# Moving the first two PSUM copies of each down-projection ahead of the silus, and the rotary tables to a later place in the code

## The chip, the cores and the metric

The kernel runs on one core of a Trainium2 chip. The metric is device time in microseconds (us). The time before is a median of 2068.57 us over three runs (2067.76 to 2076.04). A profiled execution of the same program took 2069.25 us; the profile's span, from the first instruction to the last, is 2067.5 us of it.

The core's engines work side by side, each through a list of its own in order: PE multiplies matrices into PSUM, ACT (ScalarE) and DVE (VectorE) work element by element, SP issues the loads. An engine waits for another one by a semaphore, and whatever stands behind the waiting instruction on that engine waits with it.

## The reference

One encoder layer over 256 positions of width 2048, in float32: a half-step SwiGLU feed-forward, a mixer (Fourier branch and grouped attention with a rotation of q and k), and a second half-step feed-forward.

```python
def _swiglu(x, w_gate, w_up, w_down):
    return (jax.nn.silu(x @ w_gate) * (x @ w_up)) @ w_down

h = x + 0.5 * rms_norm(swiglu(rms_norm(x, pre_g), w_gate, w_up, w_down), post_g)   # D_FF = 5632
h = h + rms_norm(merge(gates, attention(u), fourier(u)) @ w_out, post_g)           # u = rms_norm(h); u @ w_in
y = h + 0.5 * rms_norm(swiglu(rms_norm(h, pre_g2), ...), post_g2)
```

## The kernel before

**Precision and weights.** Each float32 matrix is split in two parts, hi and lo, and a product takes three matmuls (L108 to L110: hi·hi, lo·hi, hi·lo). A *piece* of weights is 128x1024: SP loads it into `raw`, ACT copies it to `whi` (L102), DVE subtracts to get `wlo` (L103).

**A round of the feed-forward.** The 5632 inner columns are cut in 11 blocks of 512. The first two are done plainly. The other nine, in each of the two feed-forwards, are rounds: 18 rounds in all. A round has two parts.

- `swiglu` multiplies the 256 tokens (two halves t = 0 and 1) with the gate and up columns of the block. Five of the eight pairs of row blocks use seven products instead of eight, with sums on DVE (`seven`, L557); three are plain. Nine partial results lie in PSUM: `p1, p5, p7` in one pool and `u0, g0, p6, g1, u1` in the pool `pmm`, which has five banks. At the end DVE adds them up (L562): first `x2 <- p6, x1`, then three sums with p7 and p5, then `x1 <- g0`, `x3 <- g1`, and at last the two of `u0, u1`. ACT does the silu of x1 and x3 (L570), DVE the product (L574).
- `Rows.feed` multiplies the block before (transposed, `hT`) with its rows of the down weights and adds that to `y`, in four column blocks `cb` of eight matmul triples. The sum is kept in SBUF: `seed` copies y of a column block into two PSUM banks (ACT, L640, one copy for each half t), PE adds onto them (tile `pr`), `out` copies the banks back to y (ACT, L657).

**What sets the order.** In the rounds DVE, ACT and PE keep the order of the program text. It is made by `Line`: a queue of six pieces. Each `feed` first takes the oldest piece, emits its matmuls (`use`) and the list of work that hangs on it (`then`), and then prepares the new piece (load, `whi`, `wlo`). So a piece is made ready six pieces before it is used, and the work in a `then` list stands between two of these preparations on ACT and DVE. The lists at the end of `swiglu` are `sums` (hung on the last two pieces of pair 6), `gates` (on the gate piece of pair 7) and `ups` (on its up piece). The next piece's matmuls are those of the down-projection's first column block, which need the first two copies; the call of `seed` for these stands at the end of `gates`, behind the two silus.

**Between the first feed-forward and the mixer.** `last_rows` ends the feed-forward: the norm, the residual and the first projection of the mixer, whose weights' pieces are prepared in between. After it SP loads q's and k's gains (`gq, gk`) and the cosine and sine tables (`rc, rsn`), and DVE multiplies them to the four tables `gcq, gsq, gck, gsk` (twelve small instructions, L784 and L787), which `norm_rope` reads later. Here a scheduler decides where DVE's instructions outside the hand-ordered part stand.

Of the kernel before, what the change touches and what calls it, by code (L numbers as in the profile page):

```python
# [10 lines left out]
F32 = mybir.dt.float32  # L11
# [3 lines left out]
AF = mybir.ActivationFunctionType  # L15
ALU = mybir.AluOpType
AX = mybir.AxisListType

P = 128
# [37 lines left out]
def encoder_layer(  # L57
# [48 lines left out]
    def mm3(ps, lh, ll, rh, rl, first, last, onto=False):  # L106

        T.matmul(ps, lh, rh, start=first, stop=False, skip_group_check=onto)  # L108
        T.matmul(ps, lh, rl, start=False, stop=False, skip_group_check=onto)  # L109
        return T.matmul(ps, ll, rh, start=False, stop=last, skip_group_check=onto)  # L110
# [245 lines left out]
    def cbs(a, cb):  # L356
        return a[:, cb * NB:(cb + 1) * NB]
# [175 lines left out]
    def swiglu(line, forms, w, hs, seed):  # L533


        ps, begun, x = {}, set(), {}

        def mul(n, a, b, last=False):
            if n not in ps:
                ps[n] = ptr.tile([P, NB], F32, tag="tr", name="pc") if n in ("p5", "p7", "p1") else                     pmm.tile([P, NB], F32, tag="mm", name="pc")  # L540
            mm3(ps[n][:], *a, *b, n not in begun, last)
            begun.add(n)

        def raw(pair, i):
            return raw_piece(w[pair // 2], pair % 2 * 2 + i)

        def plain(pair, i, *then):
            def use(b):
                for t in range(NT):
                    for j in range(2):  # L550
                        k = 2 * pair + j
                        mul("gu"[i] + str(t), forms.plain[k][t], b[j], k == KD - 1)

            line.feed(lambda: ring(raw(pair, i)[:]), use, *then)

        def minus(out, a, b):
            V.tensor_tensor(out=out, in0=a, in1=b, op=ALU.subtract)  # L557

        def add(out, a, b):
            if out not in x:  # L560
                x[out] = work(out)
            V.tensor_tensor(out=x[out][:], in0=ps[a][:], in1=x[b][:], op=ALU.add)  # L562

        def copy():
            x["x1"] = work("x1")
            A.activation(x["x1"][:], ps["p1"][:], AF.Copy)

        def silu(t):
            g = x["x" + "13"[t]]
            A.activation(g[:], g[:], AF.Silu)  # L570

        def times(t):
            g, up = x["x" + "13"[t]], x["x" + "25"[t]]
            V.tensor_tensor(out=up[:], in0=up[:], in1=g[:], op=ALU.mult)  # L574
            hs.append(up)

        def seven(pair, between=None, *then):
            a11, a12, na22, s1, s2, s3, s4 = forms.seven[pair]
            end = pair == BY_SEVEN[-1]
            h = {}  # L580

            def first():
                ra, rb = raw(pair, 0), raw(pair, 1)
                t = chunk.tile([P, WP, NB], F32, tag=("ch_hi", "ch_lo")[BY_SEVEN.index(pair) % 2], name="t13")
                h.update(ra=ra, rb=rb, t=t)
                minus(t[:, 0, :], ra[:, 1, :], ra[:, 0, :])
                minus(t[:, 1, :], rb[:, 0, :], ra[:, 1, :])
                b = ring(rb[:])
                minus(ra[:, 1, :], rb[:, 0, :], t[:, 0, :])
                return b  # L590

            def second():
                b = ring(h["t"][:])
                minus(h["t"][:, 0, :], h["ra"][:, 1, :], h["rb"][:, 1, :])
                return b

            def two(n, a, m, b, last):
                def use(ws):
                    mul(n, a, ws[0], last)
                    mul(m, b, ws[1], last)  # L600
                return use

            line.feed(first, two("u0", s4, "g0", a12, False))
            line.feed(second, two("p5", s1, "p7", s3, end))
            if between:
                between()
            line.feed(lambda: ring(h["ra"][:]), two("p1", a11, "p6", s2, end), *then[0:2])
            line.feed(lambda: ring(h["t"][:, 0:1, :]), lambda ws: mul("g1", na22, ws[0]), *then[2:])

        sums = [copy, lambda: add("x2", "p6", "x1"), lambda: add("x3", "p7", "x2"), lambda: add("x2", "p5", "x2"),  # L610
                lambda: add("x5", "p5", "x3")]
        gates = [lambda: add("x1", "g0", "x1"), lambda: add("x3", "g1", "x3"), lambda: silu(0), lambda: silu(1),
                 seed]
        ups = [lambda: add("x2", "u0", "x2"), lambda: times(0), lambda: add("x5", "u1", "x5"), lambda: times(1)]
        for kg in range(KD // CK):
            a, b = 2 * kg, 2 * kg + 1
            if kg == KD // CK - 1:
                seven(a, None, *sums)
                plain(b, 0, *gates)
                plain(b, 1, *ups)  # L620
            elif b in BY_SEVEN:
                seven(a)
                seven(b)
            else:
                seven(a, lambda: plain(b, 0))
                plain(b, 1)

    class Rows:
# [2 lines left out]
        def __init__(self, w, rb, y, first):  # L631
            self.w, self.rb, self.y, self.first, self.ps = w, rb, y, first, {}

        def seed(self, cb):
            if cb == D // NB:
                return
            self.ps[cb] = [pmm.tile([P, NB], F32, tag="mm", name="pr") for _ in range(NT)]
            if not self.first:
                for t in range(NT):
                    A.activation(self.ps[cb][t][:], cbs(self.y[t], cb), AF.Copy)  # L640

        def feed(self, line, ch, ahead):

            def use(b, cb, i):
                if i == 0:
                    if cb in ahead:
                        ahead[cb]()
                    self.seed(cb + 1)
                for t in range(NT):
                    for j in range(WP):  # L650
                        k = i * WP + j
                        mm3(self.ps[cb][t][:], ch[0][:, k, t * P:(t + 1) * P], ch[1][:, k, t * P:(t + 1) * P], *b[j],
                            self.first and k == 0, k == CK - 1, not self.first)

            def out(cb):
                for t in range(NT):
                    A.activation(cbs(self.y[t], cb), self.ps[cb][t][:], AF.Copy)  # L657

            for cb in range(D // NB):
                for i in range(CK // WP):  # L660
                    line.feed(lambda i=i, cb=cb: ring(raw_piece(self.w[self.rb, cb], i)[:]),
                              lambda b, i=i, cb=cb: use(b, cb, i), *([lambda cb=cb: out(cb)] if i == CK // WP - 1 else []))

    def ffn(u, rs, wg, wu, wgu, wd, yname, tail, gate0, w_next=None, early=()):
# [30 lines left out]
        with tc.manual_schedule(engines={mybir.EngineType.DVE, mybir.EngineType.Activation, mybir.EngineType.PE}):  # L695
            for f in range(PLAIN, nblk + 1):
                if f == 4:
                    norm, nxt = tail(y)

                def ahead(hs=hs, f=f):  # L700
                    chs.append(new_chunk("hT")) if f > PLAIN else None
                    turn_h(chs[-1], hs)

                before = {D // NB - 1: ahead}
                if f == PLAIN:
                    before[0] = lambda: forms.chunk(KD // CK - 1)
                if f == PLAIN:
                    rows = Rows(wd, 0, y, True)
                    rows.seed(0)
                rows.feed(line, chs[-1] if f > PLAIN else chs[0], before)  # L710
                if f < nblk:
                    hs = []
                    rows = Rows(wd, f - 1, y, False)
                    swiglu(line, forms, wgu[f - PLAIN], hs, lambda rows=rows: rows.seed(0))
            line.end()
        return last_rows(chs[-1], wd, nblk - 1, y, norm, nxt, w_next), nxt

# [59 lines left out]
    load(rc[:], rope_cos)  # L777
    load(rsn[:], rope_sin)
    tabs = {}
    for nm, g in (("q", gq), ("k", gk)):  # L780
        gc = const.tile([P, NT, HD], F32, name="gc" + nm)
        gs = const.tile([P, NT, HD], F32, name="gs" + nm)
        for t in range(NT):
            V.tensor_tensor(out=gc[:, t, :], in0=rc[:, t, :], in1=g[:], op=ALU.mult)  # L784
            v = lambda a: a.rearrange("p (a h c) -> p a h c", a=2, h=2)
            for half in range(2):
                V.tensor_tensor(out=v(gs[:, t, :])[:, :, half, :], in0=v(rsn[:, t, :])[:, :, half, :],  # L787
                                in1=v(g[:])[:, :, 1 - half, :], op=ALU.mult)
        tabs[nm] = (gc, gs)

    def norm_rope(ps, nm, t):

# [305 lines left out]
            V.tensor_tensor(out=cbs(mB[t], cb), in0=w[:], in1=cbs(mB[t], cb), op=ALU.mult)  # L1098


    pv = col_block(u, w_in, 5, between=[nxt.finish, None, lambda: fold_tokens(0)])
    for t in range(NT):
        vt = work("vt")
        A.activation(vt[:], pv[t][:], AF.Copy, scale=rs[t][:, 0:1])
# [225 lines left out]
```

## Time and profile before

| | before |
|---|---|
| median of three runs | 2068.57 us |
| profiled execution | 2069.25 us |
| its span | 2067.5 us |
| PE busy | 2007.7 us (97%) |
| DVE busy | 1711.6 us (83%) |
| ACT busy | 1329.6 us (64%) |
| waiting of PE for the copies of L640 | 40.8 us in 18 pieces |

How to read the profile. The page gives the busy time of each engine over the span. A group of instructions is one line: engine, operation, what it writes and reads, how often, busy time, the mean of one in ns, and the idle time of the engine just before them with what ended it. The view of waits sums these idle times by who waited for whom (total us, times, longest). The timeline lists instructions in order of time; a bracket at a row's end is the idle time before it and what ended that. The view by windows gives, for each stretch of time, its length, the busy time of each engine (with the number of instructions), the granted clock of PE and the load of the DMA engines. The end of a matmul is modelled: back to back, matmuls of one size start every 0.23 us and are shown 0.39 us long, so lengths of stalls are best taken from start to start.

### The profile page before, as it was taken

The page shows a single profiled execution, that of the slowest core. Times are in us where ns is not written, and L with a number is a line of the kernel's source. Part 1 is how long each engine was busy: PE and PEld are TensorE (multiplying, and loading weights), DVE is VectorE, ACT ScalarE, POOL GpSimd, SP SyncE. Part 2 cuts the span into 40 slices and gives each one's busy share as a digit, 9 for nine tenths or more (in the row PEclk, how much of TensorE's full clock was granted, in tenths as well). Part 3 has the DMA queues.
Part 4 walks back from the last instruction along what each step waited for, and adds up shares of the span by engine and source line. Part 5 has one row for each costly group of instructions (what it writes and reads, how often), then busy time and mean ns, then how long its engine had stood idle before and what let it go on. Part 6 is the DMA issues. An engine that isn't in the chain of part 4 may idle for free.

```text
span 2067.5 us, 26007 instructions
## 1 busy us (share of the span) xinstructions
PE 2007.7 (97%) x9200; PEld 1659.1 (80%) x9200; DVE 1711.6 (83%) x2298; ACT 1329.6 (64%) x1898; POOL 28.6 (1%) x30
## 2 busy tenths in 40 slices
PE   9999999999999999999999999999999999999998
PEld 7887777877778778888888888888778777877776
DVE  6898888888888788887877895877888889888885
ACT  7566666666666856556666654665666666666666
POOL 0000000000000010100000000000000000000002
PEclk9999999999999999999999999999999999999999
DMA  8675565555655686964555557556665566555653
GB/s 317 219 253 177 185 212 195 181 186 185 222 197 170 234 279 192 259 200 137 192 194 180 186 183 272 189 203 226 222 199 163 178 213 203 192 169 190 215 197 108
DMA packets 118739, 417.44 MB, mean 202 GB/s; under 512 B 12969, under 2 KB 19121, under 8 KB 116433
## 3 DMA queue, kind: packets, MB, share of 16 engines
q1 hardware_dynamic: 114256, 411.66, 59.7%
q0 software_dynamic: 4352, 4.13, 1.3%
q8 instruction: 72, 1.18, 0.2%
q14 instruction: 59, 0.48, 0.1%
HBM read 409.44 MB, written 6.29 MB: 201 GB/s over the span
## 4 chain that ended last, share of the span: by engine, by line
PE 80%; DVE 10%; DMA 3%; issue 3%; ACT 3%; SPq 0%; ACTq 0%; DVEq 0%
PE pc L109 14%; PE pc L110 14%; PE pc L108 14%; PE pr L108 11%; PE pr L110 11%; PE pr L109 11%; DVE wlo L103 6%; DVE x L562 2%; PE pt L178 2%; ACT whi L102 1%; DMA raw<-in_f_down 1%; DVE t L557 1%; DMA raw<-in_f_gu 1%; ACT x L570 1%; DMA raw<-in_w_fo 1%
## 5 line engine op out<-in xcount | busy, mean ns | idle before, releaser
L103 DVE TENSOR_TENSOR wlo<-raw,whi 128x1024 fp32r<-128x1024 f32 (+1 forms) x711 | 859.1, 1219 | 189.3 <-ACT whi L102 183.0
L102 ACT ACTIVATE whi<-raw 128x1024 fp32r<-128x1024 f32 (+1 forms) x711 | 742.2, 1055 | 341.0 <-PE pc L110 118.8
L108 PE MATMUL pc<-whi,fh 128*128 128x512 f32 x1062 | 413.1, 389 | 0.0
L109 PE MATMUL pc<-wlo,fh 128*128 128x512 f32 x1062 | 413.1, 389 | 0.0
L110 PE MATMUL pc<-whi,fl 128*128 128x512 f32 x1062 | 413.1, 389 | 0.0
L108 PE MATMUL pr<-whi,hTh 128*128 128x512 f32 x688 | 274.8, 399 | 40.8 <-ACT pr L640 40.8
L109 PE MATMUL pc<-wlo,uh 128*128 128x512 f32 x688 | 270.2, 393 | 4.0 <-DVE wlo L103 4.0
L108 PE MATMUL pc<-whi,uh 128*128 128x512 f32 x688 | 272.1, 396 | 1.2 <-ACT uh L740 1.2
L110 PE MATMUL pr<-whi,hTl 128*128 128x512 f32 x688 | 271.5, 395 | 0.0
L109 PE MATMUL pr<-wlo,hTh 128*128 128x512 f32 x688 | 270.8, 394 | 0.0
L110 PE MATMUL pc<-whi,ul 128*128 128x512 f32 x688 | 269.6, 392 | 0.0
L109 PEld LDWEIGHTS pc<-wlo,fh 128*128 128x128 f32 x1062 | 199.4, 188 | 41.5
L108 PEld LDWEIGHTS pc<-whi,fh 128*128 128x128 f32 x1062 | 199.3, 188 | 41.3
L110 PEld LDWEIGHTS pc<-whi,fl 128*128 128x128 f32 x1062 | 199.4, 188 | 41.3
L103 DVE TENSOR_TENSOR wlo<-t,whi 128x1024 fp32r<-128x1024 f32 (+1 forms) x180 | 171.7, 954 | 68.4 <-ACT whi L102 68.4
L102 ACT ACTIVATE whi<-t 128x1024 fp32r<-128x1024 f32 (+1 forms) x180 | 152.0, 844 | 93.7 <-DVE t L557 93.6
L108 PEld LDWEIGHTS pr<-whi,hTh 128*128 128x128 f32 x688 | 131.2, 191 | 74.7 <-ACT pr L640 48.4
L557 DVE TENSOR_TENSOR t<-raw 128x512 f32<-128x512 f32 x270 | 178.0, 687 | 3.1
L109 PEld LDWEIGHTS pc<-wlo,uh 128*128 128x128 f32 x688 | 129.8, 189 | 30.6 <-DVE wlo L103 5.6
L110 PEld LDWEIGHTS pr<-whi,hTl 128*128 128x128 f32 x688 | 130.8, 190 | 27.8
L109 PEld LDWEIGHTS pr<-wlo,hTh 128*128 128x128 f32 x688 | 131.3, 191 | 26.5
L108 PEld LDWEIGHTS pc<-whi,uh 128*128 128x128 f32 x688 | 129.8, 189 | 28.3 <-ACT uh L740 2.6
(331 smaller groups left out, 2183.0 us busy)
## 6 DMA issues: line engine op xcount, KB each, us to landing
raw<-in_f_gu SPq DMA_DIRECT2D x288, 512.0 KB, 4.3
raw<-in_f_down SPq DMA_DIRECT2D x176, 512.0 KB, 5.2
raw<-in_w_in SPq DMA_DIRECT2D x112, 512.0 KB, 4.7
raw<-in_f_up SPq DMA_DIRECT2D x32, 512.0 KB, 4.3
raw<-in_w_ao SPq DMA_DIRECT2D x32, 512.0 KB, 4.3
raw<-in_w_out SPq DMA_DIRECT2D x32, 512.0 KB, 4.2
raw<-in_f_gate SPq DMA_DIRECT2D x31, 512.0 KB, 5.7
fraw<-in_w_f SPq DMA_DIRECT2D x16, 512.0 KB, 5.3
```

Of the source, the lines that this page charges most:

```text
L102: a = A.activation(hi, src, AF.Copy)
L103: v = V.tensor_tensor(out=lo, in0=src, in1=hi.bitcast(F32), op=ALU.subtract)
L108: T.matmul(ps, lh, rh, start=first, stop=False, skip_group_check=onto)
L109: T.matmul(ps, lh, rl, start=False, stop=False, skip_group_check=onto)
L110: return T.matmul(ps, ll, rh, start=False, stop=last, skip_group_check=onto)
L178: T.transpose(pt[:, j, :], src[:, j * P:(j + 1) * P], ident[:])
L557: V.tensor_tensor(out=out, in0=a, in1=b, op=ALU.subtract)
L562: V.tensor_tensor(out=x[out][:], in0=ps[a][:], in1=x[b][:], op=ALU.add)
L570: A.activation(g[:], g[:], AF.Silu)
```

## The change

It has two parts. `seed` now makes one copy, for one half t, and is called twice at the end of a round: the first call is the last entry of `sums`, the second stands in `gates` between the sums `x1 <- g0` and `x3 <- g1`, ahead of the silus. And the loop that makes the rotation's tables becomes a function `tables`, called from within the v projection's column block, in the place of a None. No instruction is added or taken away.

```diff
         sums = [copy, lambda: add("x2", "p6", "x1"), lambda: add("x3", "p7", "x2"), lambda: add("x2", "p5", "x2"),
-                lambda: add("x5", "p5", "x3")]
-        gates = [lambda: add("x1", "g0", "x1"), lambda: add("x3", "g1", "x3"), lambda: silu(0), lambda: silu(1),
-                 seed]
+                lambda: add("x5", "p5", "x3"), lambda: seed(0)]
+        gates = [lambda: add("x1", "g0", "x1"), lambda: seed(1), lambda: add("x3", "g1", "x3"),
+                 lambda: silu(0), lambda: silu(1)]
...
-        def seed(self, cb):
-            if cb == D // NB:
-                return
-            self.ps[cb] = [pmm.tile([P, NB], F32, tag="mm", name="pr") for _ in range(NT)]
+        def seed(self, cb, t):
+            self.ps[cb, t] = pmm.tile([P, NB], F32, tag="mm", name="pr")
             if not self.first:
-                for t in range(NT):
-                    A.activation(self.ps[cb][t][:], cbs(self.y[t], cb), AF.Copy)
+                A.activation(self.ps[cb, t][:], cbs(self.y[t], cb), AF.Copy)
...
-                    self.seed(cb + 1)
+                    for t in range(NT if cb + 1 < D // NB else 0):
+                        self.seed(cb + 1, t)
...
-                    swiglu(line, forms, wgu[f - PLAIN], hs, lambda rows=rows: rows.seed(0))
+                    swiglu(line, forms, wgu[f - PLAIN], hs, lambda t, rows=rows: rows.seed(0, t))
...
-    for nm, g in (("q", gq), ("k", gk)):
-        gc = const.tile([P, NT, HD], F32, name="gc" + nm)
...
+    def tables():
+        for nm, g in (("q", gq), ("k", gk)):
+            gc = const.tile([P, NT, HD], F32, name="gc" + nm)
...
-    pv = col_block(u, w_in, 5, between=[nxt.finish, None, lambda: fold_tokens(0)])
+    pv = col_block(u, w_in, 5, between=[nxt.finish, tables, lambda: fold_tokens(0)])
```

How this moves instructions. On ACT, at the end of a round, before (`x_1458` and `x_1471` are the inputs of the two silus, `pr<-y` the copies, `whi<-raw` the hi parts of pieces to come):

```order
L566 ACTIVATE x_1458<-pc 128x512
L102 ACTIVATE whi<-raw 128x1024 x2
L570 ACTIVATE x_1458<-x_1458 128x512
L570 ACTIVATE x_1471<-x_1471 128x512
L640 ACTIVATE pr<-y_934 128x512
L640 ACTIVATE pr<-y_935 128x512
L102 ACTIVATE whi<-raw 128x1024 x2
```

And the same place of the changed kernel:

```order
L566 ACTIVATE x_1458<-pc 128x512
L102 ACTIVATE whi<-raw 128x1024
L637 ACTIVATE pr<-y_934 128x512
L102 ACTIVATE whi<-raw 128x1024
L637 ACTIVATE pr<-y_935 128x512
L570 ACTIVATE x_1458<-x_1458 128x512
L570 ACTIVATE x_1471<-x_1471 128x512
L102 ACTIVATE whi<-raw 128x1024 x2
```

The first copy moved ahead of one preparation and both silus, the second ahead of both silus; the same holds for all 18 rounds. DVE's and PE's orders in the rounds are unchanged.

On DVE, in the end of the first feed-forward, before (`ca` to `cr` are the steps of the norm's inverse root, `h` and `y` the residual and the mixer's input of half 1, `wlo` a piece of the mixer's weights):

```order
L165 TENSOR_TENSOR cu<-cz 128x1
L784 TENSOR_TENSOR gcq<-rc,gq 128x128
L166 SCALAR_TENSOR_TENSOR cv<-cu,ca 128x1
L784 TENSOR_TENSOR gcq<-rc,gq 128x128
L168 SCALAR_TENSOR_TENSOR cr<-cv,cz 128x1
L103 TENSOR_TENSOR wlo<-raw,whi 128x1024
L403 SCALAR_TENSOR_TENSOR h_1977<-y_935,cr,h_1977 128x512
L787 TENSOR_TENSOR gsq<-rsn,gq 128x2x32
L417 TENSOR_TENSOR y_935<-h_1977,gpre_1981 128x512
L103 TENSOR_TENSOR wlo<-raw,whi 128x1024
L787 TENSOR_TENSOR gsq<-rsn,gq 128x2x32 x2
L103 TENSOR_TENSOR ul_6427<-pt,uh_6426 128x512
```

And of the changed kernel:

```order
L165 TENSOR_TENSOR cu<-cz 128x1
L785 TENSOR_TENSOR gcq<-rc,gq 128x128
L166 SCALAR_TENSOR_TENSOR cv<-cu,ca 128x1
L785 TENSOR_TENSOR gcq<-rc,gq 128x128
L168 SCALAR_TENSOR_TENSOR cr<-cv,cz 128x1
L103 TENSOR_TENSOR wlo<-raw,whi 128x1024
L403 SCALAR_TENSOR_TENSOR h_1977<-y_935,cr,h_1977 128x512
L103 TENSOR_TENSOR dps<-draw,dps 128x258
L417 TENSOR_TENSOR y_935<-h_1977,gpre_1981 128x512
L103 TENSOR_TENSOR wlo<-raw,whi 128x1024
L103 TENSOR_TENSOR dcs<-draw,dcs 128x256
L103 TENSOR_TENSOR ul_6427<-pt,uh_6426 128x512
```

The two products `gcq` stand where they stood. The ten others moved back by some rows, and in the first ones' places stand the lo parts of two Fourier constants (`dps`, `dcs`), which before came later.

More of the change, by code (lines that the diff above doesn't have):

```diff
@@ L651, in use @@
                         k = i * WP + j
-                        mm3(self.ps[cb][t][:], ch[0][:, k, t * P:(t + 1) * P], ch[1][:, k, t * P:(t + 1) * P], *b[j],
+                        mm3(self.ps[cb, t][:], ch[0][:, k, t * P:(t + 1) * P], ch[1][:, k, t * P:(t + 1) * P], *b[j],
                             self.first and k == 0, k == CK - 1, not self.first)
@@ L656, in out @@
                 for t in range(NT):
-                    A.activation(cbs(self.y[t], cb), self.ps[cb][t][:], AF.Copy)
+                    A.activation(cbs(self.y[t], cb), self.ps[cb, t][:], AF.Copy)
             for cb in range(D // NB):
@@ L708, in ffn @@
                     rows = Rows(wd, 0, y, True)
-                    rows.seed(0)
+                    for t in range(NT):
+                        rows.seed(0, t)
                 rows.feed(line, chs[-1] if f > PLAIN else chs[0], before)
@@ L779, in encoder_layer @@
     tabs = {}
-    for nm, g in (("q", gq), ("k", gk)):
-        gc = const.tile([P, NT, HD], F32, name="gc" + nm)
[L782 to L789, printed above, removed]
+    def tables():
+        for nm, g in (("q", gq), ("k", gk)):
+            gc = const.tile([P, NT, HD], F32, name="gc" + nm)
+            gs = const.tile([P, NT, HD], F32, name="gs" + nm)
+            for t in range(NT):
+                V.tensor_tensor(out=gc[:, t, :], in0=rc[:, t, :], in1=g[:], op=ALU.mult)
+                v = lambda a: a.rearrange("p (a h c) -> p a h c", a=2, h=2)
+                for half in range(2):
+                    V.tensor_tensor(out=v(gs[:, t, :])[:, :, half, :], in0=v(rsn[:, t, :])[:, :, half, :],
+                                    in1=v(g[:])[:, :, 1 - half, :], op=ALU.mult)
+            tabs[nm] = (gc, gs)
     def norm_rope(ps, nm, t):
```

## The prediction

> **What bounds the kernel now.** I read the page's first part, the view of waits, then one round's end in the timeline, engine by engine, and last the rounds by windows.
>
> ```profile
> span 2067.5 us, 26007 instructions
> PE 2007.7 (97%) x9200; PEld 1659.1 (80%) x9200; DVE 1711.6 (83%) x2298; ACT 1329.6 (64%) x1898; POOL 28.6 (1%) x30
> ```
>
> PE is the bound: only 60 us of the span are left that it doesn't fill. Who holds it in these 60 us (total, times, longest):
>
> ```profile
> DVE wlo L103 <- ACT whi L102: 266.0, 232, 3.6
> ACT whi L102 <- PE pc L110: 127.3, 133, 3.0
> ACT whi L102 <- PE pr L110: 75.6, 73, 3.1
> ACT x L570 <- DVE x L562: 67.1, 18, 4.3
> PE pr L108 <- ACT pr L640: 40.8, 18, 2.9
> PE pc L109 <- DVE wlo L103: 4.0, 3, 3.4
> ```
>
> Two rows are PE's. 40.8 us are 18 waits, one a round, for the copies that this change moves; 4.0 us are nearly one wait of 3.4 us, for a lo part. The second and third row matter as much: ACT waits 206 times for PE to free a buffer of the ring. So at those points the preparation of the weights is as far ahead as the six pieces allow.
>
> One round's end, PE, then ACT, then DVE:
>
> ```profile
> 421.08 0.39 PE L110 MATMUL pc<-whi,fl 128*128 128x512 f32 x1
> 423.58 0.50 PE L108 MATMUL pr<-whi,hTh 128*128 128x512 f32 x1 [2.12 <-ACT pr L640]
> 423.92 0.39 PE L109 MATMUL pr<-wlo,hTh 128*128 128x512 f32 x1
> ```
>
> ```profile
> 415.04 0.58 ACT L566 ACTIVATE x<-pc 128x512 f32<-128x512 f32 x1
> 415.51 1.05 ACT L102 ACTIVATE whi<-raw 128x1024 fp32r<-128x1024 f32 x1
> 418.05 1.06 ACT L102 ACTIVATE whi<-raw 128x1024 fp32r<-128x1024 f32 x1 [1.48 <-DMA raw<-in_f_down]
> 421.81 1.23 ACT L570 ACTIVATE x<-x 128x512 f32<-128x512 f32 x2 [2.71 <-DVE x L562]
> 422.95 1.10 ACT L640 ACTIVATE pr<-y 128x512 f32<-128x512 f32 x2
> ```
>
> ```profile
> 416.31 0.68 DVE L562 TENSOR_TENSOR x<-pc,x 128x512 f32<-128x512 f32 x1
> 418.04 2.01 DVE L562 TENSOR_TENSOR x<-pc,x 128x512 f32<-128x512 f32 x3
> 419.96 1.22 DVE L103 TENSOR_TENSOR wlo<-raw,whi 128x1024 fp32r<-128x1024 f32 x1
> 421.10 1.28 DVE L562 TENSOR_TENSOR x<-pc,x 128x512 f32<-128x512 f32 x2
> 425.06 1.23 DVE L103 TENSOR_TENSOR wlo<-raw,whi 128x1024 fp32r<-128x1024 f32 x1 [2.69 <-ACT whi L102]
> ```
>
> The last up matmul starts at 421.08, the first of the down-projection at 423.58. Between them ACT does nothing from 419.1 to 421.8 because a silu at its head waits for the sum of g0; then come two silus (1.23 us) and only then the copies, whose banks (those of p6 and g0) had been read by DVE at 417.0 and 421.7.
>
> **Part one, the copies.** The first copy now stands behind the preparation of 415.51. Its bank is empty at 416.99 (end of the first DVE row), so it runs from 417.0 to 417.6, inside the 1.48 us that ACT waited for a load. Without that cover the next preparation slips by at most 0.58 us, and its lo part on DVE starts only at 419.96: 0.85 us behind the preparation's end at 419.11. The first copy costs nothing.
>
> The second copy waits for the sum of g0, the first of two in the row of 421.10, so until 421.74. That is a new wait on ACT, with the silus and two preparations behind it. It takes no longer than the silu's own wait at the same place. It ends at 421.8 + 0.58, and PE sees it 0.05 us later (422.95 + 0.58 against 423.58): 422.45. PE's down-projection can start at 421.08 + 0.23 = 421.31 with half 0 and needs the second bank six matmuls later, at 422.67. That leaves 0.2 us.
>
> What the wait costs today, start to start: 423.58 - 421.08 - 0.23 = 2.27 us, and 0.11 us for the slow restart (423.92 comes 0.34 us after, not 0.23). Eighteen times: 40.9 + 2.0 us. The waits differ: 18 times the 2.12 of this row are 38.2 of the 40.8 us, so 2.6 us are lateness of DVE's sums in five or six rounds. Lateness beyond the 0.2 us of slack stays as a wait for the second copy; I keep 1.6 us of it and gain 1.0.
>
> Then the clock. The rounds by windows, and some windows of 3.41 us:
>
> ```profile
> 423.58:488.78 65.20, 63.07 (x282) 52.01 (x282) 56.78 (x66) 43.78 (x56) 0.00 (x0) 1.00 0.58 193
> 553.99:620.81 66.82, 64.70 (x281) 53.13 (x282) 56.88 (x66) 43.78 (x56) 0.00 (x0) 0.97 0.57 190
> 288.98:292.39 3.41, 1.29 (x6) 1.05 (x6) 0.97 (x2) 3.01 (x5) 0.00 (x0) 1.00 0.86 321
> 292.39:295.81 3.42, 3.42 (x9) 2.63 (x8) 3.12 (x4) 2.35 (x5) 0.00 (x0) 0.50 0.30 67
> ...
> 1551.91:1555.33 3.42, 3.42 (x10) 2.64 (x9) 3.00 (x4) 2.38 (x4) 0.00 (x0) 0.50 0.20 47
> 2012.71:2016.12 3.41, 3.41 (x9) 2.68 (x9) 3.30 (x5) 2.52 (x5) 0.00 (x0) 0.50 0.34 107
> ...
> 224.13:227.54 3.41, 1.58 (x7) 1.32 (x8) 0.72 (x3) 3.35 (x6) 0.00 (x0) 1.00 0.81 287
> ```
>
> After five of the 18 waits (at 291, 554, 1551, 1814 and 2011; three of the windows behind them are shown) the granted clock is 0.50 for 3.41 us, and the round takes 66.82 instead of 65.20: 1.62 us each, 8.1 in all. The window of 288.98, in which PE worked 1.29 us, is followed by one; that of 224.13 with 1.58 us is not. It is the wait that does it, where it falls into one such window. Without waits this goes too.
>
> [...]
>
> **Does the rest keep up?** After the change PE is 2.4 us earlier, ACT only the 0.5 us of one copy gone from behind the silus. So the preparations and DVE start the down-projection 1.9 us late against PE. They make it up before it is needed:
>
> ```profile
> 436.38 1.23 DVE L103 TENSOR_TENSOR wlo<-t,whi 128x1024 fp32r<-128x1024 f32 x1 [1.08 <-ACT whi L102]
> 441.39 0.69 DVE L103 TENSOR_TENSOR wlo<-t,whi 128x512 fp32r<-128x512 f32 x1 [1.55 <-ACT whi L102]
> 443.85 1.06 ACT L102 ACTIVATE whi<-raw 128x1024 fp32r<-128x1024 f32 x1 [1.52 <-PE pr L110]
> 456.62 2.35 DVE L103 TENSOR_TENSOR wlo<-raw,whi 128x1024 fp32r<-128x1024 f32 x2
> 458.84 0.39 PE L109 MATMUL pc<-wlo,fh 128*128 128x512 f32 x1
> ```
>
> DVE idles 1.08 and 1.55 us, ACT then waits 1.52 us for PE to free a buffer. At that point both are again tied to PE, as before. The tightest piece of the round comes later: ready at about 457.8, used at 458.84, 1.0 us to spare, and its chain begins at the wait of 443.85, so it keeps its distance. DVE's work in a round is 56.8 us against PE's 62.8 (65.20 less 2.4).
>
> **Part two, the tables.** DVE and ACT at the end of the first feed-forward, and the window that follows:
>
> ```profile
> 739.74 0.16 DVE L165 TENSOR_TENSOR cu<-cz 128x1 f32<-128x1 f32 x1
> 742.56 0.29 DVE L784 TENSOR_TENSOR gcq<-rc,gq 128x128 f32<-128x128 f32 x1 [2.66 <-DMA rc<-in_rope_cos]
> 744.38 0.80 PE L109 MATMUL pc<-wlo,uh 128*128 128x512 f32 x1 [3.40 <-DVE wlo L103]
> 748.83 0.69 DVE L103 TENSOR_TENSOR ul<-pt,uh 128x512 fp32r<-128x512 f32 x1 [1.70 <-ACT uh L102]
> 743.31 0.42 ACT L102 ACTIVATE dps<-draw 128x258 fp32r<-128x258 f32 x1 [7.41 <-DMA draw<-in_dft_pos]
> 742.95:749.78 6.83, 5.40 (x15) 4.36 (x16) 5.13 (x11) 2.78 (x8) 0.00 (x0) 0.50 0.95 253
> ```
>
> The first product `gcq` waits 2.66 us for the cosines, the lo part behind it comes late, and PE stands 3.40 us and then runs at half clock. Moving the loop in the text should cure that. But in the changed order both `gcq` stand at the same place, still behind `cu` and ahead of that lo part, with the same load to wait for. What moved are the ten others, and they were not in the way. I give this part 0. In their place `dps` comes ahead of `y`: its hi part is ready at 743.73, DVE gets there at 745, and 0.42 us instead of 0.22 stand before `y`; the 0.2 is covered because PE, at half clock, comes to the transposes of y a microsecond later. `dcs` falls into the 1.70 us before the row of 748.83. On SP a spill changes place with a load and one small load now waits for `dps`; the pieces behind it are used some 10 us later. The bounds: 0.84 us lost (both lo parts uncovered), or, if the wait for the cosines does go, a gain of 3.55 us (the 3.40 from start to start) and half of 5.40, together 6.2.
>
> **The sum.** 40.9 + 2.0 + 1.0 + 8.1 = 52.0 us. From 2069.25 of the profiled execution: 2017.2. The median lies 0.7 us below the profiled time, so **2016.5 us**. Half a per cent, 10 us, is about what a measurement of this kernel can tell from no change.
>
> **Rivals.**
>
> *The half-clock windows stay.* If they belong to the phase of the clock's window and not to the waits, 8.1 us are not gained: 2024.6. For it: only five of eighteen waits show one. Against: each follows a wait directly, and 1.29 against 1.58 us of work separates them. 7%. [...]
>
> *The tables do leave the path.* If the cosines land earlier against PE, the wait at 742.56 goes: 2016.5 - 6.2 = 2010.3. For it: SP's later rows are in another order. Against: all loads ahead of `rc` stand as they did. 7%.
>
> *DVE becomes the bound of a round.* Its 8.4 us of idle time (65.20 - 56.78) may not shrink by 2.4: if half of it is the fixed handing to and fro with ACT (266 us of waits for `whi` over the program), a round comes down by only 1.2 us, and the gain is 18 x 1.2 + 8.1 = 30: 2039. For it: those waits are the largest row of the view. Against: the spare 1.0 us at the tightest piece, and ACT's waits for PE. 10%.
>
> *Slower: the new loads' lateness at the round's end.* With shorter rounds the down weights come at a higher rate; the preparation of 418.05 already waits for its load. Each us that this load lands later passes through the lo part (419.96) and the sum of g0 to the second copy and to PE, once 0.85 and 0.2 us of slack are used up. A round loses from 2.4 + 1.05 = 3.5 us of lateness on. At 5 us in every round: 18 x 1.5 = 27 us less the clock's 8, or about 2087. For it: 321 GB/s in the window of 288.98. Against: a DMA share of 0.58 over a round, which becomes 0.60. 4%.
>
> **Chances and range.** The forecast 72%, the rivals 7, 7, 10 and 4. The range takes in the first two rivals: 2009 to 2027 holds 86%, a little over the 8 in 10 wanted. Faster by over 0.5% (below 2058): 0.93; within: 0.04; slower: 0.03.
>
> **What would show it.** In the profile after: the row "PE pr L108 <- ACT pr" falls from 40.8 to about 2 us; rounds of 62.8 us; no 0.50 in the clock at a round's end; DVE's busy time unchanged; ACT's wait for DVE at the silus passes to the copies. The wait of `gcq` for the cosines is still there, and PE's 3.4 us with it. A new wait of PE for `wlo` in the rounds would mean that DVE has become the bound; one for the copies of over 1 us, that a sum is late.

## The result and the profile after

The changed kernel took 2017.32 us, median of four executions (2015.35 to 2019.71), against 2068.16 us of the kernel before measured beside it: a ratio of 0.9748, 95% interval 0.9719 to 0.9776. Forecast were 2016.5 us, with a range of 2009 to 2027. The profiled execution took 2019.0 us.

The first lines of its page:

```profile
span 2017.2 us, 25972 instructions
PE 1997.5 (99%) x9200; PEld 1654.6 (82%) x9200; DVE 1707.8 (85%) x2298; ACT 1323.2 (66%) x1898; POOL 28.6 (1%) x30
```

The span is 50.3 us shorter. PE's busy time fell by 10 us only, DVE's and ACT's hardly at all: what went is idle time of PE. The waits (total us, times, longest), first of all engines, then PE's own:

```profile
DVE wlo L103 <- ACT whi L102: 217.6, 192, 3.6
ACT whi L102 <- PE pc L110: 127.9, 132, 3.0
ACT whi L102 <- PE pr L110: 73.0, 53, 3.1
ACT pr L637 <- DVE x L562: 71.1, 45, 3.5
...
PE pc L109 <- DVE wlo L103: 3.9, 3, 3.3
PE pa L926 <- DVE zl L103: 1.5, 1, 1.5
PE pr L108 <- ACT pr L637: 0.4, 2, 0.2
```

PE's 40.8 us of waiting for the copies are down to 0.4. ACT's wait for DVE at the end of a round is still there, 71.1 us where the silus had 67.1; it now stands ahead of the copies. The 3.9 us for a lo part, in the middle of the block, are what they were (4.0).

One round's end after the change, PE, ACT and DVE:

```profile
409.60 0.39 PE L110 MATMUL pc<-whi,fl 128*128 128x512 f32 x1
409.82 0.39 PE L108 MATMUL pr<-whi,hTh 128*128 128x512 f32 x1
...
411.19 0.40 PE L108 MATMUL pr<-whi,hTh 128*128 128x512 f32 x1
```

```profile
405.55 0.60 ACT L637 ACTIVATE pr<-y 128x512 f32<-128x512 f32 x1 [0.46 <-DVE x L562]
406.08 1.04 ACT L102 ACTIVATE whi<-raw 128x1024 fp32r<-128x1024 f32 x1
410.34 0.60 ACT L637 ACTIVATE pr<-y 128x512 f32<-128x512 f32 x1 [3.21 <-DVE x L562]
410.87 1.14 ACT L570 ACTIVATE x<-x 128x512 f32<-128x512 f32 x2
```

```profile
408.49 1.22 DVE L103 TENSOR_TENSOR wlo<-raw,whi 128x1024 fp32r<-128x1024 f32 x1
409.62 1.28 DVE L562 TENSOR_TENSOR x<-pc,x 128x512 f32<-128x512 f32 x2
```

The last up matmul starts at 409.60 and the down-projection at 409.82, with no gap. The first copy was done at 406.15. The second starts right behind the sum of g0 (409.62, the first of the two in that row), ends at 410.94, and its bank is written by PE from 411.19.

The program by windows, the kernel before and then the kernel after. Each window runs from the start of one round's down-projection to that of another: eight rounds of the first feed-forward; its last round, the mixer and the second feed-forward up to its first round; eight rounds of the second. The columns are length, busy time of PE, its weight loads, DVE, ACT and POOL, granted clock of PE, share and rate of the DMA engines.

```profile
160.78:686.00 525.22, 507.86 (x2249) 418.27 (x2249) 454.62 (x528) 350.16 (x441) 0.00 (x0) 0.99 0.58 192
686.00:1484.85 798.85, 789.33 (x3797) 657.15 (x3797) 639.38 (x988) 489.29 (x801) 17.66 (x16) 1.00 0.64 209
1484.85:2011.27 526.42, 507.84 (x2248) 418.20 (x2248) 455.07 (x528) 349.87 (x441) 0.00 (x0) 0.99 0.59 192
```

```profile
158.38:661.75 503.37, 503.19 (x2249) 416.35 (x2248) 452.96 (x528) 347.70 (x440) 0.00 (x0) 1.00 0.60 201
661.75:1459.01 797.26, 789.91 (x3798) 657.32 (x3797) 639.11 (x990) 488.72 (x800) 17.66 (x16) 1.00 0.65 209
1459.01:1962.27 503.26, 503.17 (x2250) 416.27 (x2248) 452.91 (x528) 347.55 (x440) 0.00 (x0) 1.00 0.61 200
```

So the 50.3 us are: 2.4 ahead of the first window (160.78 against 158.38, the first round's stall), 21.85 and 23.16 in the rounds, 1.6 in the middle, 1.3 behind the last window. PE's idle time in the rounds is 0.18 and 0.09 us where it was 17.4 and 18.6; the clock is whole there.

The middle gave 1.6 us although the stall at the head of its last part (3.13 us from start to start before, 0.23 now, and the slow restart, 0.34 us to the next matmul instead of 0.23) should alone have given 3.0. The places, DVE first, then PE, then three windows of 3.41 us:

```profile
718.28 0.29 DVE L785 TENSOR_TENSOR gcq<-rc,gq 128x128 f32<-128x128 f32 x1 [3.01 <-DMA rc<-in_rope_cos]
720.10 0.79 PE L109 MATMUL pc<-wlo,uh 128*128 128x512 f32 x1 [3.26 <-DVE wlo L103]
726.62 0.63 PE L178 MATMUL pt<-ident,y 128*128 128x128 f32 x4 [0.37 <-DVE y L417]
902.58 0.33 PE L926 MATMUL pa<-odd,zl 128*126 128x130 f32 x1 [1.54 <-DVE zl L103]
...
719.88:723.29 3.41, 3.19 (x9) 2.50 (x10) 3.25 (x6) 1.85 (x6) 0.00 (x0) 0.50 0.79 174
900.79:904.20 3.41, 1.87 (x20) 1.73 (x19) 2.71 (x5) 1.03 (x2) 0.00 (x0) 1.00 0.75 237
904.20:907.61 3.41, 3.41 (x10) 2.74 (x10) 3.34 (x8) 1.27 (x4) 0.00 (x0) 0.50 0.51 154
```

The wait for the cosines is where it was; the half-clock stretch behind it is one window long instead of two (6.83 us before). New are 0.37 us at a transpose, and 1.54 us at 902.58 with a half-clock window behind it.

### The profile page after: what moved, and what is told of

Read it like the earlier page. It is cut to its first block, busy times and chain, and to the rows that moved or that the text cites. A ratio compares the mean times of both kernels' runs of the same rounds, so it can differ in the third digit from the quotient of the medians.

```text
span 2017.2 us, 25972 instructions
## 1 busy us (share of the span) xinstructions
PE 1997.5 (99%) x9200; PEld 1654.6 (82%) x9200; DVE 1707.8 (85%) x2298; ACT 1323.2 (66%) x1898; POOL 28.6 (1%) x30
## 4 chain that ended last, share of the span: by engine, by line
PE 89%; DVE 7%; DMA 2%; ACT 1%; issue 1%; SPq 0%; DVEq 0%; ACTq 0%
PE pc L109 17%; PE pc L108 17%; PE pc L110 17%; PE pr L108 11%; PE pr L110 11%; PE pr L109 11%; DVE wlo L103 4%; PE pt L178 2%; DMA raw<-in_f_down 1%; DVE t L557 1%; ACT whi L102 1%; DMA raw<-in_w_fo 1%; DMA rc<-in_rope_cos 0%; PE pe L108 0%; PE pe L109 0%
## 5 line engine op out<-in xcount | busy, mean ns | idle before, releaser
L108 PE MATMUL pr<-whi,hTh 128*128 128x512 f32 x688 | 270.6, 393 | 0.5 <-ACT pr L637 0.4
L110 PEld LDWEIGHTS pc<-whi,ul 128*128 128x128 f32 x688 | 130.0, 189 | 27.0
```

## The experiments

Every ratio below is against the kernel before, run on the same chip in the same turn. All kernels compute the whole layer.

**Each part alone.** One kernel has only the copies (`seed`, `sums`, `gates`), one only `tables`; the changed kernel ran once more beside them. The diff of the second against the kernel before:

```diff
-    for nm, g in (("q", gq), ("k", gk)):
...
+    def tables():
+        for nm, g in (("q", gq), ("k", gk)):
...
-    pv = col_block(u, w_in, 5, between=[nxt.finish, None, lambda: fold_tokens(0)])
+    pv = col_block(u, w_in, 5, between=[nxt.finish, tables, lambda: fold_tokens(0)])
```

> The changed kernel once more, on the chip of the next three, as their yardstick and for a second trace. Expected 2015 to 2020 us. Two things of its first trace are looked at again: the wait of PE for the second copies (0.5 us in all there) and two events in the middle, 1.54 us of waiting for a Fourier lo part behind a late load of w_fo, followed by 3.41 us at half clock. If these belong to the change they come again; if a load was late by chance in that execution, they don't.

> The copies ahead of the silus, the tables made where they were. Theory (the copies are the whole gain, the tables give nothing because gcq stands where it stood): 2017 us, within 2 of the changed kernel, with the same wait of PE behind gcq (3.2 to 3.4 us). Rival (the tables' move gives what its place suggests): 2023 us, 6 more than the changed kernel.

> The tables as in the change, the copies where they were. Theory: 2068 us, no difference from before, PE's wait behind gcq at 3.2 to 3.4 us and 40.8 us of waits for the copies. Rival: 2062 us.

Measured: the change 2016.43 us (0.9741, interval 0.9724 to 0.9758); the copies alone 2017.17 (0.9746, 0.9724 to 0.9767); the tables alone 2070.38 (1.0004, 0.9991 to 1.0017). The whole gain is the copies'. A row of the waits of the kernel with the tables alone, and one of PE's waits of the kernel with the copies alone:

```profile
PE pr L108 <- ACT pr L640: 41.1, 18, 3.0
...
PE pc L109 <- DVE wlo L103: 3.1, 2, 2.7
```

The tables alone leave the 18 waits as they are (41.1 us, before 40.8). And without the tables' move the wait in the middle is 2.7 us; with it, it is 3.26 us in the change's first trace and 4.84 in its second. In these three DVE's order from `cu` to that lo part is the same, and PE's wait goes with DVE's own wait for the cosines (2.05, 3.01 and 4.07 us).

**The second copy behind the silus.** The place of the first copy is kept, the second goes back.

```diff
-        gates = [lambda: add("x1", "g0", "x1"), lambda: seed(1), lambda: add("x3", "g1", "x3"),
-                 lambda: silu(0), lambda: silu(1)]
+        gates = [lambda: add("x1", "g0", "x1"), lambda: add("x3", "g1", "x3"),
+                 lambda: silu(0), lambda: silu(1), lambda: seed(1)]
```

> The changed kernel with the second copy of each round put back behind the silus; the first stays early. By the working of the prediction the second copy starts when the silus end (1.14 us later than in the kernel before minus one copy, at 422.95 on its clock), is seen by PE at 423.58, and is needed at 422.67: a wait of 0.91 us in each round plus about 0.1 for the restart, 18 x 1.0 = 18 us: 2035 us (2031 to 2038). The waits are 0.9 us, so by the threshold read from the trace (1.83 us idle in a window of 3.41 is harmless, 1.97 is not) no half-clock window follows. Rival A, only the first copy matters because PE has half 0 to do meanwhile: 2017. Rival B, the two copies count alike: halfway, 2043. Rival C, short waits trip the clock too: 5 windows of 1.62 us more, 2043, and 0.50 in the clock at some rounds' ends.

Measured: 2037.64 us (0.9843, 0.9825 to 0.9860). PE's waits and one regular round:

```profile
PE pr L108 <- ACT pr L637: 16.6, 18, 1.3
...
222.19:286.02 63.83, 63.07 (x282) 52.00 (x281) 56.77 (x67) 43.71 (x55) 0.00 (x0) 1.00 0.59 199
```

The wait comes back in all 18 rounds, but now at the matmul that needs the second bank, six matmuls into the down-projection. A regular round takes 63.83 us, 1.04 more than the 62.79 of the change. There is no half-clock window behind any of the 18 waits: each is shorter (at most 1.3 us) than those of before (at least 2.1). So moving the first copy alone is worth 30.5 us (2068.16 or 2069.17 less 2037.64, by either measurement of before within a us), and the second copy's move the other 20: 18 times about 1.1.

**The second copy one sum later.** It stands behind `x3 <- g1` in the list.

```diff
-        gates = [lambda: add("x1", "g0", "x1"), lambda: seed(1), lambda: add("x3", "g1", "x3"),
-                 lambda: silu(0), lambda: silu(1)]
+        gates = [lambda: add("x1", "g0", "x1"), lambda: add("x3", "g1", "x3"), lambda: seed(1),
+                 lambda: silu(0), lambda: silu(1)]
```

> The changed kernel with the second copy behind both gate sums (in ACT's order still ahead of the silus; it now waits for a point one DVE sum later, or rather stands behind nothing else new). If ACT's copy waits only for the bank of g0, as its data do, nothing changes: 2017 us. If it is held until the sum of g1 (422.38 on the clock of the round before the change), it ends at 423.0 and PE sees it 0.38 us late, 0.45 with the restart: 18 x 0.45 = 8, so 2025 us. The runs of the changed kernel without this edit are at 2016 to 2017.

Measured: 2018.15 us (0.9746, 0.9732 to 0.9760), and 1.8 us of PE's wait for the copies: no difference from the change that this measurement can tell. The second copy of one round in this kernel:

```profile
410.36 0.60 ACT L637 ACTIVATE pr<-y 128x512 f32<-128x512 f32 x1 [3.21 <-DVE x L562]
```

It starts when it did in the change (410.34, after 3.21 us of idle time there too). The sums are on DVE and the copy on ACT, so the place in the list does not set when the copy starts; its own data do, and that is the sum of g0. What counts on ACT is that no silu stands ahead of it.

**A longer wait, for the clock.** Half-clock windows stood behind five of the eighteen waits of the kernel before. If the idle time does it, a longer wait must have more of them. This kernel is the one before with two more copies on ACT ahead of the moved ones, of `x1` onto itself.

```diff
+        def idle_copy():
+            A.activation(x["x1"][:], x["x1"][:], AF.Copy)
...
-                 seed]
+                 idle_copy, idle_copy, seed]
```

> The kernel before, with two more copies of a tile onto itself on ACT between the silus and the first copies: PE's wait grows by about 1.1 us, from 2.1 to 3.2 us, in all 18 rounds. It computes the same. For all theories the waits themselves cost 18 x 1.1 = 20 us: 2089 us. Theory (a window of 3.41 us with more than about 1.85 us of idle time trips the clock for the next window): a wait of 3.2 us leaves less than that in both windows it touches only if it is split nearly evenly, about one time in seven, so some 15 of 18 waits are followed by half clock instead of 5 or 6, 10 x 1.62 = 16 us more: about 2105 us. Rival (a whole window has to be idle): no more half-clock windows than before, 2089. Rival (the windows come by their phase, whatever the wait): 5 or 6 as before, 2089.

Measured: 2109.68 us (1.0190, 1.0176 to 1.0204). PE's waits, and by windows a round with a half-clock window, one without, and the two windows of 3.41 us behind the wait at 432.73:

```profile
PE pr L108 <- ACT pr L643: 61.9, 18, 4.2
...
1778.32:1846.29 67.97, 64.67 (x282) 53.24 (x282) 56.88 (x66) 45.13 (x58) 0.00 (x0) 0.97 0.57 186
1711.94:1778.32 66.38, 63.08 (x281) 51.99 (x281) 56.79 (x66) 44.84 (x58) 0.00 (x0) 1.00 0.58 190
430.08:433.50 3.42, 0.77 (x3) 0.67 (x4) 0.27 (x1) 3.39 (x7) 0.00 (x0) 1.00 0.62 213
433.50:436.91 3.41, 3.41 (x9) 2.65 (x8) 2.66 (x4) 2.71 (x4) 0.00 (x0) 0.50 0.13 30
```

Sixteen of the 18 waits are now followed by a half-clock window, where five were. A round with one takes 67.97 us, one without 66.38: 1.59 us, much like the 1.62 before. The longer waits (61.9 less 40.8 us) and eleven more windows of 1.6 us than in the trace of before make 38.7 us; the medians differ by 39.1 (2109.68 against 2070.59 of the kernel before in that turn). The rule "the clock's phase does it, not the wait" is out.

**The loads of the tables later.** To ask what the wait in the middle is worth, the loads of `gq, gk, rc, rsn` were moved into `tables`, so that nothing of theirs stands near the norm's steps.

```diff
-    gq, gk = work("gq", [P, HD]), work("gk", [P, HD])
-    load(gq[:], q_g.partition_broadcast(P))
...
     def tables():
+        gq, gk = work("gq", [P, HD]), work("gk", [P, HD])
+        load(gq[:], q_g.partition_broadcast(P))
...
```

> The changed kernel, with the four loads of gains, cosines and sines moved into the function of the tables, so that they are issued behind the second spill. In its order the products gcq now stand some 40 rows later; but in their old place among the steps of the norm's root stand the lo parts of two Fourier constants, whose loads move up in the queue into the place of the gains' loads. Theory (whatever stands there and depends on a load holds the piece behind it): the first lo part is ready at about 740.4 on the clock of before instead of 742.6, the piece comes about 1.1 us earlier, PE's wait falls from 3.3 to about 2.2 us: 2014.5 to 2016. Rival (the cosines alone were late): the wait goes, 2011 to 2013.

Measured: 2015.97 us (0.9737, 0.9724 to 0.9751), no gain that can be told from the change. The wait has not gone. DVE, ACT and PE:

```profile
716.20 0.43 DVE L103 TENSOR_TENSOR dps<-draw,dps 128x258 fp32r<-128x258 f32 x1 [1.70 <-ACT dps L102]
715.75 0.42 ACT L102 ACTIVATE dps<-draw 128x258 fp32r<-128x258 f32 x1 [4.16 <-DMA draw<-in_dft_pos]
719.53 0.50 PE L109 MATMUL pc<-wlo,uh 128*128 128x512 f32 x1 [2.86 <-DVE wlo L103]
```

With `gcq` gone the scheduler put the split of the constant `dps` into its place, ahead of the norm's steps and of the same lo part, and that waits for the next load in SP's list.

**Tables and constants later.** As above, and the loads and splits of the Fourier constants (`dps, dcs, odd, first, alt, mid`) go behind the transposes of k, in the third gate.

```diff
+    def constants():
+        nonlocal dps, dcs, odd, first, alt, mid
...
-    gate(12, mB, 2, at=folds_at(4), between=[lambda t=t: turn_k(t) for t in range(NT)])
+    gate(12, mB, 2, at=folds_at(4), between=[lambda t=t: turn_k(t) for t in range(NT)] + [lambda: constants()])
```

> As the one before, and the Fourier constants too are loaded and split later, in the gate block 12. Now nothing that depends on a load of its own stands among the steps of the root. The piece behind them begins at about 740.4 on the clock of before and is ready at 741.6, needed at 740.8: PE waits 0.8 us instead of 3.3, and no half-clock window follows. Gain 2.5 + 1.7 = 4 us on the changed kernel: 2013 us (2011 to 2015), faster than both kernels. Rival: the tables' loads, issued later, now hold DVE in the v projection, where the ring of pieces gives some us of cover; then PE waits there instead, and the time stays at 2016 to 2018.

Measured: 2022.11 us (0.9777, 0.9760 to 0.9793): not the 2013 us expected, but about 5 us above the change's medians of 2016.43 and 2017.32. The wait at 718 fell to 0.42 us and the clock stayed whole there. But in the gate, ACT and PE:

```profile
846.39 0.42 ACT L102 ACTIVATE dps<-draw 128x258 fp32r<-128x258 f32 x1 [4.98 <-DMA draw<-in_dft_pos]
...
852.21 1.06 ACT L102 ACTIVATE whi<-fraw 128x1024 fp32r<-128x1024 f32 x1 [1.35 <-DVE fraw L892]
853.32 0.80 PE L108 MATMUL pe<-whi,ueh 128*128 128x260 f32 x2 [6.47 <-ACT whi L102]
```

ACT now waits 4.98 us for the constants' load with a piece of weights behind it, and PE 6.47 us for that piece. In both places tried, a load that is issued just ahead of its use made the engine wait (4.16 and 4.98 us).

**Loads far ahead.** So the loads, not the products, must move. The two gains, both tables and the two large constants are loaded in the first feed-forward, when `tail` is called, into the three buffers of `xpool`, which stand empty until the mixer. The change ran once more beside it.

```diff
+    def preload():
...
+            xt = xpool.tile([P, sum(n for _, n, _ in tile)], F32, tag="xt", name="pre")
...
+                load(pre[nm], src)
...
     def tail(y):
+        preload()
         for t in range(NT):
...
-    split(dps[:, 0, :], dps[:, 1, :], constant(dft_pos, WE + WO)[:])
+    split(dps[:, 0, :], dps[:, 1, :], pre["dp"])
```

> The change, with the loads of the two gains, the two rotation tables and the two constants dps and dcs (six DMAs, about 0.6 MB) made in the first feed-forward part, some 650 us ahead of their use, into buffers that stand empty there; their products and splits (12 + 2 on VectorE, 2 on ScalarE) then stand there too. If the wait of TensorE in the middle of the block (2.9 to 4.8 us in the runs so far, wherever the tables and constants were made) is the lateness of these loads and nothing else: the wait at 718 to 723 is under 0.5 us, no window at half clock there, the 0.3 us at the transposes after it gone as well; 2012 to 2013 against 2016.4 to 2017.3 of the change. Rival 1, the cost returns at the start: VectorE is busy 24.57 of the 25 us from 50 to 75, and the 14 instructions (about 3.3 us) stand there; a wait on weight splits appears at 55 to 90 us and the time is about 2015. Rival 2, the next late load (the constants of ones, a weight) takes its place as it did in the two runs before: a wait of 2 to 3 us at 720 to 727, time 2016 to 2017.

> The change once more, beside the run with the early loads on the same chip: 2016 to 2017.5 by every theory, with 2.5 to 5 us of wait of TensorE at 718 to 723.

Measured: 2013.04 us (0.9727, 0.9712 to 0.9742), the change beside it 2015.70 us (0.9744, 0.9730 to 0.9758). All five executions of the first (2010.56 to 2013.47) lie below all four of the second (2015.16 to 2016.83); by their means and spread the ratio of the two is 0.9984, 95% interval 0.9976 to 0.9992. It is faster than both kernels. The scheduler put splits and products at 80 to 88 us, and between the norm's steps nothing is left. PE's waits for lo parts, the longest of them, DVE at the old place, and two of the moved products:

```profile
PE pc L109 <- DVE wlo L103: 1.4, 3, 0.5
...
716.77 0.50 PE L109 MATMUL pc<-wlo,uh 128*128 128x512 f32 x1 [0.53 <-DVE wlo L103]
...
715.04 0.16 DVE L165 TENSOR_TENSOR cu<-cz 128x1 f32<-128x1 f32 x1
715.23 0.16 DVE L166 SCALAR_TENSOR_TENSOR cv<-cu,ca 128x1 f32<-128x1 f32 x1
...
85.41 0.29 DVE L797 TENSOR_TENSOR gcq<-pre 128x128 f32<-128x128 f32 x1
85.62 0.36 DVE L800 TENSOR_TENSOR gsq<-pre 128x64 f32<-128x64 f32 x2
```

The longest wait is 0.53 us (2.05 in the change beside it, 3.26 and 4.84 in its other traces), and no half-clock window stands there. The small wait at the transposes was expected to go and did not: it is 0.41 us, at 722.32. The first round's down-projection starts at 158.28 us, not later than the change's 158.38, 158.30 and 159.00: the start paid nothing. The gain of 2.7 us is less than the 4 expected. In its one trace the change beside it had the shortest wait of the three, with no half-clock window behind it; that fits the smaller gain, but its other executions have no trace.

## Why the prediction was right, point by point

*The first copy is free.* Right. It runs at 405.55, behind 0.46 us of wait for the sum that empties its bank, and the preparation behind it is ready long before DVE comes to it at 408.49.

*The second copy has 0.2 us to spare.* Right: it ends at 410.94, PE would see it at 410.99 (it came 0.05 us behind the copy before, 422.95 + 0.58 against 423.58) and needs it at 411.19. With the copy behind the silus the slack is overdrawn by 1.04 us a round, which the experiment showed.

*40.9 + 2.0 us of stalls and slow restarts.* Right. In all 18 rounds the step from the last up matmul to the down-projection is 0.23 us.

*1.0 us of lateness gained, 1.6 kept.* Nearly. The rounds of the two windows last 503.37 and 503.26 us, 16 times 62.79 are 1004.64: 1.99 us are left. Most of them stand where the prediction said, at the matmul of the second bank in the rounds whose sum is late:

```profile
536.68 0.60 ACT L637 ACTIVATE pr<-y 128x512 f32<-128x512 f32 x1 [3.48 <-DVE x L562]
536.76 0.39 PE L110 MATMUL pr<-whi,hTl 128*128 128x512 f32 x1
537.33 0.50 PE L108 MATMUL pr<-whi,hTh 128*128 128x512 f32 x1 [0.18 <-ACT pr L637]
```

Here the step is 0.57 instead of 0.23 us. The view of waits shows only 0.18 of it. Over all 18 rounds these steps are 1.5 us too long, close to the 1.6 kept; the matmul behind each of the eight late ones comes 0.11 us late too, 0.9 us in all, which the prediction did not count.

*8.1 us of clock.* Right in kind and size: no half-clock window is left at a round's end, and the longer wait had sixteen. The rival by which the windows stay is out. Nor was PE idle for a whole window: in the five that tripped at the rounds' ends before it worked 1.09 to 1.44 us of the 3.41, and in that of 430.08 with the longer wait 0.77 us.

*DVE and ACT keep up.* Right. DVE works 56.6 us in a round (452.96 / 8) of 62.9, and PE is idle for 0.18 us in eight of them. The rival of a DVE-bound round is out: DVE's waits for `whi` fell from 266.0 to 217.6 us with the rounds, so they were no fixed cost.

*The tables give nothing.* Right by the runs of each part (1.0004, and 0.9746 without them against 0.9741 with them), and for the reason given: `gcq` waits for the cosines as before, 3.01 us, and PE 3.26.

Two small steps failed. "The 0.2 is covered" was wrong: PE waits 0.37 us for `y` at 726.62. It does so by 0.29 us with the copies alone too, so the order of `dps` is not all of it. And the sum held the rest of the middle for unchanged. It lost 1.4 us, and these are most of what the profiled execution lacks (50.3 us of the 52.0 forecast): DVE waited 1.26 us for a load of `w_fo`, PE waited 1.54 us at 902.58 for the lo part behind it, and a half-clock window followed. In the change's two other traces that wait is 0.81 and 0.27 us, without such a window, so it varies between executions of the same kernel; why the load came later in the first is not shown. The bound of 6.2 us for a wait for the cosines that goes was too high for the median: with the loads far ahead 2.7 us came.

The slower rival did not show: the loads take 0.60 of the DMA engines' time in a round, as worked out, and no round's stall came back.

## What to carry to other kernels

Where an engine takes work in its order, put what another engine needs next ahead of what nobody waits for yet, and look up, for each of two like copies, when its own bank is free and its own reader comes: here one could go almost six microseconds earlier for nothing (on the clock of before 417.0 instead of 422.95) and the other had to stand exactly behind the sum. In these runs a stall of the matrix engine cost 1.6 us more than its length when it filled more than about 55% of one of the clock's windows of 3.41 us: eighteen stalls of 0.8 to 1.3 us tripped none, five of eighteen of 2.1 to 2.9 us did, and sixteen of eighteen of 3.3 to 4.2 us. So, by these runs, a stall of 2 us can cost more than two of 1 us. The late loads were cured by loading earlier; moving their consumers only moved the wait, or let the scheduler put the next load's consumer into the gap.

## What the runs showed of the hardware that was not expected

How much idle time was followed by half clock can be read closely. The half-clock windows of a trace stand on a grid: those at 292.39 and 555.22 in the kernel before begin 262.83 us apart, 77 lengths of 3.41 us. On this grid, PE's idle time in each window was taken from its matmul records, over the traces of before, of the change and of all experiments. Among windows of 512-wide matmuls at full clock, none with up to 1.86 us idle was followed by half clock (eleven lie between 1.54 and 1.86), and of those with 1.91 us or more all were, but for one, itself of 1.91. In the kernel before, the six windows of 1.97 to 2.32 us were followed, the two of 1.82 and 1.83 us not. So in these traces the point lay near 1.9 us, about 55% of the window. At the rounds' ends each cost 1.6 us (1.62 in the kernel before, 1.59 with the longer wait). The two windows next to the point, in the kernel with the longer wait (full clock behind it) and with the tables alone (half clock behind it):

```profile
1710.08:1713.49 3.41, 1.55 (x7) 1.30 (x8) 0.07 (x1) 3.38 (x7) 0.00 (x0) 1.00 0.33 127
682.45:685.87 3.42, 1.51 (x7) 1.25 (x8) 0.73 (x3) 3.28 (x6) 0.00 (x0) 1.00 0.70 276
```

At half clock less was enough: two such windows with 1.43 us idle (742.95 in the kernel before) and 1.13 us (719.54 with the second copy one sum later) were followed by another at half clock. One with 0.22 us (719.88 in the change) was not.

At full clock, too, it isn't idle time alone. Two windows that tripped had only 1.54 and 1.55 us idle: that of 900.79 above, which held 20 matmuls, most of them only 130 wide, and one at 945.50 in the kernel with the longer wait, at the same place of the program. Why these tripped was not tried.
